# One prefetch moved, weight copies kept at other uses: eight-core macaron encoder block on Trainium2

## The chip, the cores and the metric

The kernel runs on all 8 cores of one Trainium2 chip. Each core computes one of 8 sequences by itself, with its own copy of all weights; nothing is exchanged. The metric is the device time of the slowest core, in microseconds (us). Most executions agree within 0.3%. Some fall into a second, slower state, in which the cores of one die, sometimes of both, run at a lower granted TensorE clock (0.86 in one run of the changed kernel, 0.995 to 0.998 in its others); those are left out ("fast runs" below are the others). PE is the matmul engine, DVE and ACT the vector and scalar engines, POOL and SP two further engines; here POOL issues the DMA transfers that convert f32 to bf16 on the way ("casting loads"), SP the plain ones.

## The reference, cut to what matters

```python
# x: (8, 4096, 1024) float32; D_FF = 2816, D_IN = 4608
x = x + 0.5 * swiglu(rmsnorm(x, norm_ffn1), ffn1_w_gate, ffn1_w_up, ffn1_w_down)
h = rmsnorm(x, norm_mix)
z = h @ w_in                                # q, k, v | u, v_s | gate logits
...                                         # chunked attention, spatial gating
merged = g_att * (y_att @ w_branch_att) + g_sgu * (y_sgu @ w_branch_sgu)
x = x + merged @ w_out
x = x + 0.5 * swiglu(rmsnorm(x, norm_ffn2), ffn2_w_gate, ffn2_w_up, ffn2_w_down)
return rmsnorm(x, norm_final)
```

## The kernel before

A core works through 8 tiles of 512 tokens; all matmuls are bf16. The weights do not fit into the on-chip memory. They stream through one ring buffer (RING, 46 groups of 512 columns, so about five or six chunks of up to 1 MB) in the order in which they are used. In DRAM they are f32. The first uses of a chunk load it from f32 through POOL's casting queue (1 MB written for 2 MB read). At one of these uses, which the table KEEP_AT names, the bf16 chunk is also written back from the ring to DRAM; every later use loads that copy, a plain 1 MB transfer in SP's queue. A slot of the ring is free only when its matmuls *and* its write-back are done.

```python
F2 = (3, 8, 9, 10, 2, 0, 1, 4, 5, 6, 7)     # order of the gate/up chunks
def _keep_at():                             # the use (0 = first) at which the bf16 copy is written
    at = {("ffs", 0, f2): int(n < 4) for n, f2 in enumerate(F2J)}   # gate/up of feed-forward 1
    at |= {("wds", 0, d): 1 for d in range(8)}                      # its down weights
    at |= {("wis", g): n for g, n in zip((4, 3, 2, 0, 1), (1, 0, 1, 0, 1))}     # projection
    at |= {("mgs", d): n for d, n in enumerate((0, 1, 1, 2, 0, 1, 2, 1))}       # merge
    at |= {("wos", 0): 1, ("wos", 1): 2}
    at |= {("ffs", 1, f2): n for f2, n in zip(F2, (1, 2, 0, 2, 1, 2, 1, 0, 2, 1, 2))}
    ...
def pump():                                 # issues loads while the ring has room
    ...
    if any(a < o + ng and o < b for a, b in live.values()):
        return                              # no room: the queue stops here
    ...
    if chunk not in converted:
        p.dma("pool", lambda e: e.dma_start(out=o, in_=i_), writes=res, ...)     # cast from f32
        if u >= KEEP_AT[chunk]:
            converted.add(chunk)
            pending_wb[k] = (chunk, scr, dst, i)                     # write-back follows
    else:
        p.dma("sp", lambda e: e.dma_start(out=dst, in_=scr), ...)    # the bf16 copy
```

x of a tile is 2 MB of f32, in two halves in SP's queue. The parts of the schedule that the change touches (pieces of work are yielded; a "hook" runs at a numbered piece):

```python
def dense_bank():                           # PSUM banks in turn
    b = dn[0] % n_dense[0]; dn[0] += 1
    return b
...
def down_last(t, i, fac):                   # last down product; tokens split at T_A = 320
    for d in range(2):      block(d, ALL);      nsq(t, d)
    for d in range(2, 8):   block(d, parts[0]); nsq(...)
    for d in range(2, 8):
        block(d, parts[1]); ...             # norm, apply, store of parts[0] in between
    nstat(sl=parts[1])                      # the very last norm
    ...
# main program, tile 0
run_all(main)                               # down product of tile 1 beside attention of tile 0
load_x(2)                                   # x of tile 2, ahead of the merge
...
merge(t, mh, HT, ht_m)
wh = {}                                     # hooks of the second input projection
...
win(t + 1, wh)
run_all(ffn(t, 1, False, ffn2_hooks(t)))    # second feed-forward of tile 0, all weights from f32
# next iteration: main = ffn(2, 0, ...): first feed-forward of tile 2, needs x of tile 2
```

The first feed-forward of tiles 0 and 1 is computed together, chunk by chunk, so tile 2's is only the *second* use of its weights.

Of the kernel before, what the change touches and what calls it, by code (L numbers as in the profile page):

```python
# [18 lines left out]
NT = S_LEN // T  # L19
NGR = 46  # L20
NSEM = 12
T_A = 320
N_WARM = 7
EPS = 1e-6
R_MAX = 1e18
# [7 lines left out]
def _keep_at():  # L33

    at = {("ffs", 0, f2): int(n < 4) for n, f2 in enumerate(F2J)}
    at |= {("wds", 0, d): 1 for d in range(8)}
    at |= {("wis", g): n for g, n in zip((4, 3, 2, 0, 1), (1, 0, 1, 0, 1))}
    at |= {("mgs", d): n for d, n in enumerate((0, 1, 1, 2, 0, 1, 2, 1))}
    at |= {("wos", 0): 1, ("wos", 1): 2}
    at |= {("ffs", 1, f2): n for f2, n in zip(F2, (1, 2, 0, 2, 1, 2, 1, 0, 2, 1, 2))}  # L40
    at |= {("wds", 1, d): n for d, n in enumerate((1, 2, 2, 1, 0, 2, 1, 2))}
    return at
# [173 lines left out]
def build_nc(n_tiles=NT):  # L216
# [28 lines left out]
    with ExitStack() as st:  # L245
# [63 lines left out]
        def run(p, dry):  # L309
# [222 lines left out]
            def store(t, d, sl=ALL, queue="sp"):  # L532
                b = t % 3
                h = int(sl.start > 0)
                p.dma(queue, lambda e: e.dma_start(out=out_d[t][:, d:d + 2, sl], in_=X[b][:, d:d + 2, sl]),
                      reads=[("X", b, d), ("X", b, d + 1)], writes=[("outd", d, h)], sem=f"o{d}{h}")
# [129 lines left out]
            def down_last(t, i, fac):  # L666


                b3 = t % 3
                parts = (slice(0, T_A), slice(T_A, T))  # L670
                W = [None] * 8

                def block(d, sl):
                    if not W[d]:
                        W[d] = get_slot(("wds", i, d))
                    w, wres, k = W[d]
                    by = dense_bank()
                    for fc in range(NFC):
                        p.add("pe", lambda e, fc=fc: e.matmul(  # L679
                            bank(by)[:, sl], lhsT=w[:, fc * 128:(fc + 1) * 128], rhs=HT[:, fc, sl],  # L680
                            start=(fc == 0), stop=(fc == NFC - 1)),
                            reads=wres + [("HT", fc)], writes=[rb(by)])
                    xs = X[b3][:, d, sl]
                    p.add("dve", lambda e: e.scalar_tensor_tensor(
                        out=xs, in0=bank(by)[:, sl], scalar=fac, in1=xs, op0=ALU.mult, op1=ALU.add),
                        reads=[rb(by), ("X", b3, d)], writes=[("X", b3, d)])
                    if sl.stop == T:
                        free_slot(k)

                for d in range(2):  # L690
                    block(d, ALL)
                    nsq(t, d)
                for d in range(2, 8):
                    block(d, parts[0])
                    nsq(t, d, "dve" if d > 5 else "pool", parts[0])
                for d in range(2, 8):
                    block(d, parts[1])
                    if d == 2:
                        nstat(sl=parts[0])
                    nsq(t, d, "dve" if d > 5 else "pool", parts[1])  # L700
                    if d > 2:
                        for j in range(2):
                            if 2 * (d - 3) + j < 8:
                                napply(t, 3, 2 * (d - 3) + j, parts[0])
                        if d < 7:
                            store(t, 2 * (d - 3), parts[0])
                nstat(sl=parts[1])
                for d in range(8):
                    napply(t, 3, d, parts[1])
                    if d % 2:  # L710
                        store(t, d - 1, parts[1], ("sp", "act")[d // 2 % 2])

            def ffn(t, i, use_tanh, hooks=None, narrow=False, last=False):
                hook = Hooks(hooks)
                for f2 in F2:
                    yield from gu_chunk(t, f2, get_slot(("ffs", i, f2)), "tanh" if use_tanh else "silu", hook,
                                        by_k=last and f2 == F2[0])
                if last:
                    down_last(t, i, 0.5)
                else:  # L720
                    yield from down(t, i, 0.25 if use_tanh else 0.5, hook, narrow=2 * narrow)
# [366 lines left out]
            def add_hook(hk, n, *fns):  # L1088
                hk[n] = chain(*(([hk[n]] if n in hk else []) + list(fns)))
# [14 lines left out]
            def both_hooks():  # L1104
# [5 lines left out]
                add_hook(hk, 48, const_ops)  # L1110
                return hk

            def ffn1_hooks(t):
                hk = {D1 - 2: ln_table}
                finish_hooks(hk, t - 2, 1)
                for d in range(8):
                    add_hook(hk, D1 + SQ_AT[d], P(nsq, t, d))
                return hk

            def ffn2_hooks(t):  # L1120
                hk = {}
                if t + 1 < n_tiles:
                    for s in range(4):
                        add_hook(hk, 8, P(sgu_pe, s, 4 + s))
                        add_hook(hk, 9 + 3 * s, P(sgu_out, s, 4 + s))
                if t + 2 < n_tiles:
                    for d in range(8):
                        add_hook(hk, 10 + 3 * d, P(nsq, t + 2, d, "dve" if t == 0 else "pool"))
                    add_hook(hk, 40, nstat)
                    for d in range(8):  # L1130
                        add_hook(hk, D1 + d, P(napply, t + 2, 0, d))
                if t == n_tiles - 2:
                    add_hook(hk, D1 - 2, ln_table)
                if t == n_tiles - 1:
                    for d in range(8):
                        add_hook(hk, 4 + 2 * d, P(nsq, t - 1, d))
                    finish_hooks(hk, t - 1, 22)
                    add_hook(hk, 38, flag_ops)
                if t < n_tiles - 2:
                    for d in range(8):  # L1140
                        add_hook(hk, D1 + SQ_AT[d], P(nsq, t, d))
                return hk
# [17 lines left out]
            for d in range(8):  # L1160
                add_hook(hk, SQ_AT[d], P(nsq, 0, d, "dve"))
            run_all(down(0, 0, 0.5, Hooks(hk)))
            hk = {0: nstat}
            for d in range(8):
                add_hook(hk, 1 + d // 4 * 2, P(napply, 0, 1, d))
            add_hook(hk, 3, lambda: p.add("dve", lambda e: e.tensor_copy(out=RSTD[:], in_=RS[1]),
                                          reads=[("RS", 1)], writes=["RSTD"]))
            run_all(gu_chunk(1, F2J[-1], get_slot(("ffs", 0, F2J[-1])), "raw", Hooks(hk), ht_second))
# [9 lines left out]
            for t in range(n_tiles):  # L1178
                last = t == n_tiles - 1
                mh = {}  # L1180
                if not last:
                    if t == 0:
                        main = second
                        n_dense[0] = 2
                        interleave(main, attention(t), 25, n_att(t))
                    else:
                        main = ffn(t + 1, 0, True, ffn1_hooks(t + 1), narrow=True)
                        interleave(main, attention(t), N_FFN + 16 - 3, n_att(t), 2 * NFC)
                    run_all(main)
                    if t == 0 and n_tiles > 2:  # L1190
                        load_x(2)
                    add_hook(mh, 0, nstat)
                    for d in range(8):
                        add_hook(mh, 1 + d // 2, P(napply, t + 1, 1, d))
                for d in range(8):
                    add_hook(mh, ("o", d), P(nsq, t, d))
                if last:
                    n_dense[0] = 4
                    add_hook(mh, ("o", 0), ln_table)
                    merge(t, mh, XT[(t - 1) % 2], lambda dc: ("XT", (t - 1) % 2, dc))  # L1200
                    for _ in range(3):
                        next(last_ffn)
                    nstat()
                    for d in range(8):
                        napply(t, 2, d)
                    run_all(last_ffn)
                else:
                    merge(t, mh, HT, ht_m)
                    wh = {}
                    add_hook(wh, 1, nstat)  # L1210
                    for d in range(8):
                        add_hook(wh, 3 + 2 * d, P(napply, t, 2, d))
                    win(t + 1, wh)
                if t == n_tiles - 2:
                    last_ffn = ffn(t, 1, True, ffn2_hooks(t), narrow=True)
                    interleave(last_ffn, attention(t + 1), N_FFN + 16 - 8, n_att(t + 1), 2 * NFC)
                else:
                    run_all(ffn(t, 1, False, ffn2_hooks(t), last=last))
# [122 lines left out]
```

## Time and profile before

| | before |
|---|---|
| time, median of 3 runs | 2743.96 us (2743.35 to 2861.79, the highest a slow one) |
| spans of the 8 cores in the profiled run | 2732.9 (core 3) to 2743.7 us (core 4) |
| PE busy, core 4 | 2693.3 us, 98% |
| longest wait of PE | 11.7 us, for the first weights of the second input projection |

Here is one more view, busy time by stretch, of core 3 of the kernel before. Its columns are: stretch and length; busy us (and instructions) of PE, PE's weight loads, DVE, ACT, POOL; mean granted clock of PE; mean busy share of the 16 DMA engines (in this view a full stretch shows slightly over 1); GB/s.

```profile
216.00:256.00 40.00, 38.58 (x201) 17.01 (x199) 17.79 (x36) 12.74 (x20) 7.26 (x16) 1.00 1.02 204
...
298.00:340.00 42.00, 42.00 (x196) 18.98 (x194) 22.34 (x34) 16.69 (x22) 2.18 (x4) 1.00 1.01 195
340.00:354.00 14.00, 13.28 (x61) 5.71 (x59) 6.02 (x10) 4.41 (x7) 7.82 (x8) 1.00 0.71 193
354.00:389.00 35.00, 32.19 (x150) 14.61 (x151) 12.57 (x23) 12.65 (x19) 5.23 (x11) 1.00 1.02 225
...
505.00:550.00 45.00, 44.65 (x208) 20.10 (x207) 22.56 (x34) 11.68 (x17) 1.14 (x2) 1.00 1.04 274
```

The last column but one is the one to read. From 216 to 550 us the DMA engines are full on this core but for 14 us in which they are at 0.71 (the stretches left out here show 1.01 to 1.03). In this stage, from the end of the joint first feed-forward to the first feed-forward of tile 2, weights are cast from f32 and written back at the same time.

### The profile page before, as it was taken

The page shows a single profiled execution, that of the slowest core. Times are in us where ns is not written, and L with a number is a line of the kernel's source. Part 1 is how long each engine was busy: PE and PEld are TensorE (multiplying, and loading weights), DVE is VectorE, ACT ScalarE, POOL GpSimd, SP SyncE. Part 2 cuts the span into 40 slices and gives each one's busy share as a digit, 9 for nine tenths or more (in the row PEclk, how much of TensorE's full clock was granted, in tenths as well). Part 3 has the DMA queues.
Part 4 walks back from the last instruction along what each step waited for, and adds up shares of the span by engine and source line. Part 5 has one row for each costly group of instructions (what it writes and reads, how often), then busy time and mean ns, then how long its engine had stood idle before and what let it go on. Part 6 is the DMA issues. An engine that isn't in the chain of part 4 may idle for free.

```text
span 2743.7 us, 38774 instructions; the slowest of 8 cores (2732.9 to 2743.7 us)
## 1 busy us (share of the span) xinstructions
PE 2693.3 (98%) x13174; PEld 1223.2 (45%) x13174; DVE 1180.8 (43%) x1931; ACT 911.0 (33%) x1483; POOL 336.4 (12%) x395
## 2 busy tenths in 40 slices
PE   8999989999999999999999999999999999999997
PEld 3444434444444444444444444444444444444445
DVE  5445533445334453344533445324544245454432
ACT  3313432234322343224432243322532225424321
POOL 4101120101211011110011001010010101100111
PEclk9999999999999999999999999999999999999999
DMA  9979999967797456973344634446344443443352
GB/s 190 200 128 197 193 191 180 223 226 163 181 207 234 151 153 169 241 239 134 135 154 146 215 130 139 153 146 210 132 142 152 152 171 133 146 149 127 133 185 86
DMA packets 92503, 461.95 MB, mean 168 GB/s; under 512 B 9608, under 2 KB 11656, under 8 KB 62096
## 3 DMA queue, kind: packets, MB, share of 16 engines
q1 hardware_dynamic: 68896, 361.09, 38.1%
q0 software_dynamic: 22720, 97.89, 22.5%
q8 instruction: 114, 1.87, 0.3%
q14 instruction: 85, 0.70, 0.1%
q10 hardware_dynamic: 688, 0.41, 0.0%
HBM read 488.03 MB, written 65.01 MB: 202 GB/s over the span
## 4 chain that ended last, share of the span: by engine, by line
PE 92%; DMA 3%; DVE 1%; issue 1%; ACT 1%; POOL 0%; DVEq 0%; ACTq 0%; POOLq 0%; SPq 0%
PE ps L572 43%; PE ps L645 20%; PE ps L1021 7%; PE ps L755 6%; PE ps L768 4%; PE ps L1031 4%; PE ps L1050 3%; PE ps L926 2%; PE ps L903 1%; DMA mgs<-RING 1%; PE ps L679 1%; DMA RING<-mgsrc 1%; DMA RING<-wisrc 1%; DMA X<-xT 0%; ACT E L909 0%
## 5 line engine op out<-in xcount | busy, mean ns | idle before, releaser
L572 PE MATMUL ps<-XT,RING 128*128 128x512 bf16 x5632 | 1228.2, 380 | 10.9 <-DMA RING<-fsrc 4.5
L572 PEld LDWEIGHTS ps<-XT,RING 128*128 128x128 bf16 x5632 | 548.6, 98 | 681.2 <-issue 26.9
L645 PE MATMUL ps<-HT,RING 128*128 128x512 bf16 x2480 | 567.6, 379 | 0.1
L500 POOL TENSOR_TENSOR ACC<-ACC,TG 128x512 f32<-128x512 f32 (+2 forms) x177 | 227.7, 1286 | 1698.2 <-ACT TG L497 1696.4
L594 DVE TENSOR_TENSOR HT<-ps,TG 128x512 bf16<-128x512 f32 x332 | 229.2, 691 | 424.1 <-PE ps L572 360.5
L645 PEld LDWEIGHTS ps<-HT,RING 128*128 128x128 bf16 x2480 | 235.6, 98 | 286.2 <-issue 24.5
L497 ACT ACTIVATE TG<-X 128x512 f32<-128x512 f32 (+2 forms) x230 | 140.6, 615 | 328.9 <-DVE X L657 232.1
L1021 PE MATMUL ps<-XT,RING 128*128 128x512 bf16 x1024 | 242.0, 379 | 0.0
L579 ACT ACTIVATE TG<-ps 128x512 f32<-128x512 f32 x154 | 92.0, 597 | 394.4 <-PE ps L572 374.1
L585 ACT ACTIVATE TG<-ps 128x512 f32<-128x512 f32 x154 | 91.8, 597 | 365.7 <-PE ps L572 354.8
L581 DVE SCALAR_TENSOR_TENSOR TG<-TG,ps 128x512 f32<-128x512 f32 x154 | 105.8, 687 | 238.0 <-ACT TG L579 196.9
L909 ACT ACTIVATE E<-ps 128x1024 bf16<-128x1024 f32 (+3 forms) x156 | 152.8, 985 | 105.8 <-PE ps L903 102.3
L914 DVE TENSOR_TENSOR E<-E,EB 128x1024 bf16<-128x1024 bf16 (+1 forms) x240 | 119.1, 500 | 139.2 <-ACT E L909 127.9
L755 PE MATMUL ps<-XT,RING 128*128 128x512 bf16 x768 | 168.9, 379 | 0.0
L1021 PEld LDWEIGHTS ps<-XT,RING 128*128 128x128 bf16 x1024 | 99.6, 98 | 120.8 <-issue 3.2
L1035 DVE SCALAR_TENSOR_TENSOR TG<-TG,ps 128x512 f32<-128x512 f32 x128 | 87.3, 686 | 153.2 <-PE ps L1031 116.7
L657 DVE SCALAR_TENSOR_TENSOR X<-ps,X 128x512 f32<-128x512 f32 x104 | 71.7, 691 | 184.7 <-PE ps L645 183.4
L1026 ACT ACTIVATE TG<-ps,BG 128x512 f32<-128x512 f32 x128 | 87.2, 687 | 189.2 <-PE ps L1021 176.9
L523 DVE SCALAR_TENSOR_TENSOR XT<-X,G,RSTD 128x512 bf16<-128x512 f32 x176 | 124.5, 746 | 46.3 <-ACT RSTD L516 46.3
L768 PE MATMUL ps<-RING,XT 128*128 128x512 bf16 x512 | 116.1, 383 | 12.3 <-DMA RING<-wisrc 11.7
L755 PEld LDWEIGHTS ps<-XT,RING 128*128 128x128 bf16 x768 | 74.9, 98 | 90.2
L1050 PE MATMUL ps<-HT,RING 128*128 128x512 bf16 x448 | 99.0, 379 | 2.4 <-DVE HT L1040 2.4
(111 smaller groups left out, 1626.5 us busy)
## 6 DMA issues: line engine op xcount, KB each, us to landing
RING<-ffs SPq DMA_DIRECT2D x126, 1024.0 KB, 4.9
RING<-wds SPq DMA_DIRECT2D x93, 704.0 KB, 4.3
RING<-mgs SPq DMA_DIRECT2D x48, 768.0 KB, 4.2
RING<-wis SPq DMA_DIRECT2D x32, 1024.0 KB, 4.9
RING<-fsrc POOLq DMA_DIRECT2D x29, 1024.0 KB, 16.2
RING<-wd POOLq DMA_DIRECT2D x35, 704.0 KB, 15.3
ffs<-RING SPq DMA_DIRECT2D x22, 1024.0 KB, 13.0
out<-X SPq DMA_DIRECT2D x28, 512.0 KB, 5.3
```

The costliest lines, as they stand in the source:

```text
L497: p.add("act", lambda e: e.activation(out=buf[:, sl], in_=src, func=AF.Square, scale=1.0 / 32.0), reads=[xres], writes=[bres])
L500: p.add(eng, lambda e: e.tensor_tensor(out=acc, in0=acc, in1=buf[:, sl], op=ALU.add), reads=["ACC", bres], writes=["ACC"])
L523: p.add("dve", lambda e: e.scalar_tensor_tensor(out=dst, in0=src, scalar=G4[:, which * 8 + d:which * 8 + d + 1], in1=RSTD[:, sl], op0=ALU. ...
L572: p.add("pe", lambda e: e.matmul(bank(b), lhsT=Wc[:, kc * 512 + j * 128:kc * 512 + (j + 1) * 128], rhs=xt[:, kc, :], start=(kc == 0), stop ...
L594: p.add("dve", lambda e: e.tensor_tensor(out=dst, in0=bank(bu), in1=buf[:], op=ALU.mult), reads=[rb(bu), bres], writes=[dres])
L645: p.add("pe", lambda e, n=n, fc=fc, W=W, by=by, hap=hap: e.matmul(bank(by), lhsT=W[:, fc * 128:(fc + 1) * 128], rhs=hap, start=(n == 0), s ...
L755: p.add("pe", lambda e, kc=kc, W=W, b=b, cc=cc: e.matmul(bank(b), lhsT=W[:, kc * 512 + cc * 128:kc * 512 + (cc + 1) * 128], rhs=XT[t % 2][ ...
L768: p.add("pe", lambda e, kc=kc, W=W, b=b, s=s: e.matmul(bank(b), lhsT=XT[t % 2][:, kc, s * 128:(s + 1) * 128], rhs=W[:, kc * 512:(kc + 1) * ...
L909: p.add("act", lambda e, j=j, sl=sl, qa=qa, col=ok_col(): e.activation(out=E[:, sl, :, qa:T], in_=PS[1 + j][:].rearrange("p (h c) -> p h c ...
L914: p.add("dve", lambda e, sl=sl, q0=q0, q1=q1, u0=u0: e.tensor_tensor(out=E[:, sl, :, q0:q1], in0=E[:, sl, :, q0:q1], in1=EB[:, 2 * hp:2 * ...
L1021: p.add("pe", lambda e, kc=kc, W=W, bgt=bgt, j=j: e.matmul(bank(bgt), lhsT=W[:, j * 1024 + kc * 128:j * 1024 + (kc + 1) * 128], rhs=XT[t % ...
L1050: p.add("pe", lambda e, dc=dc, W=W, by=by, d4=d4: e.matmul(bank(by), lhsT=W[:, (d4 * 8 + dc) * 128:(d4 * 8 + dc + 1) * 128], rhs=m[:, dc, ...
```

## The change

Its intent: take the 11.7 us before the second projection away by moving the 2 MB of x out of the merge and by writing fewer copies there; shorten the first norm, the start of the last feed-forward and the end of the program; and give gate, up and down fixed PSUM bank parity.

```diff
-T_A = 320
+T_A = 256
+D_SPLIT = 3
...
-    at |= {("wds", 0, d): 1 for d in range(8)}
-    at |= {("wis", g): n for g, n in zip((4, 3, 2, 0, 1), (1, 0, 1, 0, 1))}
-    at |= {("mgs", d): n for d, n in enumerate((0, 1, 1, 2, 0, 1, 2, 1))}
+    at |= {("wds", 0, d): int(d > 3) for d in range(8)}
+    at |= {("wis", g): n for g, n in zip((4, 3, 2, 0, 1), (0, 1, 1, 0, 1))}
+    at |= {("mgs", d): n for d, n in enumerate((1, 2, 1, 2, 3, 1, 2, 3))}
...                                     # down_last: 3 columns whole, then 5 twice in halves
             def ffn(t, i, use_tanh, hooks=None, narrow=False, last=False):
                 hook = Hooks(hooks)
+                if narrow:
+                    dn[0] += (2 - dn[0]) % 4
...
-                        add_hook(hk, 10 + 3 * d, P(nsq, t + 2, d, "dve" if t == 0 else "pool"))
+                        add_hook(hk, 10 + 3 * d if t else 20 + 2 * d, P(nsq, t + 2, d, ...))
...
-            hk = {0: nstat}             # first half kernel: norm one group later
+            hk = {1: nstat}
...
-                    if t == 0 and n_tiles > 2:
-                        load_x(2)
...
+                    silu_table()        # last feed-forward: table early, six PSUM banks
+                    next(last_ffn)
...
+                    n_dense[0] = 6
...
                     for d in range(8):
                         add_hook(wh, 3 + 2 * d, P(napply, t, 2, d))
+                    if t == 0 and n_tiles > 2:
+                        add_hook(wh, 8, P(load_x, 2))
                     win(t + 1, wh)
```

More of the change, by code (lines that the diff above doesn't have):

```diff
@@ L688, in block @@
                         free_slot(k)
-                for d in range(2):
+                for d in range(D_SPLIT):
                     block(d, ALL)
                     nsq(t, d)
-                for d in range(2, 8):
+                for d in range(D_SPLIT, 8):
                     block(d, parts[0])
                     nsq(t, d, "dve" if d > 5 else "pool", parts[0])
-                for d in range(2, 8):
+                for d in range(D_SPLIT, 8):
                     block(d, parts[1])
-                    if d == 2:
+                    if d == D_SPLIT:
                         nstat(sl=parts[0])
                     nsq(t, d, "dve" if d > 5 else "pool", parts[1])
-                    if d > 2:
-                        for j in range(2):
-                            if 2 * (d - 3) + j < 8:
-                                napply(t, 3, 2 * (d - 3) + j, parts[0])
-                        if d < 7:
-                            store(t, 2 * (d - 3), parts[0])
+                    if d > D_SPLIT:
+                        for j in (0, 1):
+                            napply(t, 3, 2 * (d - D_SPLIT - 1) + j, parts[0])
+                        store(t, 2 * (d - D_SPLIT - 1), parts[0])
                 nstat(sl=parts[1])
@@ L1111, in both_hooks, with silu_table @@
                 return hk
+            def silu_table():
+                p.add("act", lambda e: e.activation(out=ASTAT[:, 3:4], in_=EPSB[:], func=AF.Silu),
+                      reads=["EPSB"], writes=[("as", 3)])
             def ffn1_hooks(t):
@@ L1127, in ffn2_hooks @@
                     for d in range(8):
-                        add_hook(hk, 10 + 3 * d, P(nsq, t + 2, d, "dve" if t == 0 else "pool"))
+                        add_hook(hk, 10 + 3 * d if t else 20 + 2 * d, P(nsq, t + 2, d, "dve" if t == 0 else "pool"))
                     add_hook(hk, 40, nstat)
@@ L1131, in ffn2_hooks @@
                         add_hook(hk, D1 + d, P(napply, t + 2, 0, d))
-                if t == n_tiles - 2:
+                if t >= n_tiles - 2:
                     add_hook(hk, D1 - 2, ln_table)
@@ L1162, in run @@
             run_all(down(0, 0, 0.5, Hooks(hk)))
-            hk = {0: nstat}
+            hk = {1: nstat}
             for d in range(8):
-                add_hook(hk, 1 + d // 4 * 2, P(napply, 0, 1, d))
+                add_hook(hk, 3, P(napply, 0, 1, d))
             add_hook(hk, 3, lambda: p.add("dve", lambda e: e.tensor_copy(out=RSTD[:], in_=RS[1]),
@@ L1203, in run @@
                     nstat()
-                    for d in range(8):
+                    silu_table()
+                    next(last_ffn)
+                    for d in range(7):
                         napply(t, 2, d)
                     run_all(last_ffn)
+                    napply(t, 2, 7)
+                    n_dense[0] = 6
                 else:
```

## The prediction

> **What bounds the kernel now.** I read the busy shares first. PE is busy 98% of a span of 2743.7 us on the slowest core, so all that any reordering can win is the other 2%: 2743.7 - 2693.3 = 50.4 us, part of it a start and an end that no kernel avoids.
>
> ```profile
> PE 2693.3 (98%) x13174; PEld 1223.2 (45%) x13174; DVE 1180.8 (43%) x1931; ACT 911.0 (33%) x1483; POOL 336.4 (12%) x395
> ```
>
> The second line of the chain that ended last says that this is not an accident of one window: 43% of the span is the gate and up product (L572), 20% the down product (L645), and DMA only 3%.
>
> Next the waits of PE (who released it, us in total, times, longest). The reader is to see that a single wait is 11.7 us, that one of three is 4.8 us, and that the rest is crumbs.
>
> ```profile
> PE ps L768 <- DMA RING<-wisrc: 11.7, 1, 11.7
> PE ps L512 <- DVE ACCR L503: 6.6, 3, 4.8
> PE ps L903 <- ACT E L909: 4.6, 8, 0.6
> ...
> PE ps L572 <- ACT TG L585: 1.5, 1, 1.5
> PE ps L572 <- DVE X L657: 1.5, 2, 1.3
> ```
>
> Then PE's timeline (start, us, what, idle before it) to place them. The 11.7 us stand at the head of the second input projection; 1.60 us in the first half kernel; 1.26, 0.22 and 1.52 us at the start of the last feed-forward; 4.82 us before the very last norm.
>
> ```profile
> 207.37 0.47 PE L512 MATMUL ps<-ACCR,ONESR 128*128 128x512 f32 x1 [1.60 <-DVE ACCR L503]
> ...
> 366.20 5.07 PE L768 MATMUL ps<-RING,XT 128*128 128x512 bf16 x16 [11.73 <-DMA RING<-wisrc]
> ...
> 2612.37 0.38 PE L572 MATMUL ps<-XT,RING 128*128 128x512 bf16 x1 [1.26 <-DVE X L657]
> 2612.96 6.42 PE L572 MATMUL ps<-XT,RING 128*128 128x512 bf16 x29 [0.22 <-DVE X L657]
> 2620.91 32.97 PE L572 MATMUL ps<-XT,RING 128*128 128x512 bf16 x152 [1.52 <-ACT TG L585]
> ...
> 2734.68 0.50 PE L512 MATMUL ps<-ACCR,ONESR 128*128 128x192 f32 x1 [4.82 <-DVE ACCR L503]
> ```
>
> Where the 11.7 us come from is in the chain of waits, in order of time. A merge load ends at 313; the write-back of that same merge weight (its bf16 copy, to DRAM) takes 35 us; only then is its ring slot free and the weights of the projection can be loaded, another 17 us.
>
> ```profile
> 287.77 25.51 DMA RING<-mgsrc
> 313.34 35.11 DMA mgs<-RING
> 349.04 16.93 DMA RING<-wisrc
> ```
>
> The write-back is 768 KB; elsewhere such a chunk lands in 4.2 us. Ahead of it in SP's queue stand the two 1 MB loads of x of tile 2, issued at 298.6, which took 37.6 us. The DMA table for 240 to 480 us shows why: the engines are full, 80.3% of their time in POOL's casting loads and 18.3% in SP's queue.
>
> **What the Trainium skill says.** "TensorE: Matmul & The Clock Gate", section "Single matmul latency", gives about 216 ns between matmuls of 512 columns. The trace agrees: 72.54 us for 336 of them, 215.9 ns. So PE's work is at its floor. "DMA: Bandwidth & Descriptors", section "Queues, rings and completion order", says that each engine goes round its queues packet by packet and takes one ring's descriptors in order. The trace agrees: at 300 to 312 us POOL's queue has 86.1% and SP's 15.0%, and the write-back ends after the x loads ahead of it. "ScalarE: Activation LUTs", section "What ACT_TABLE_LOAD costs", has 1283 ns for a load plus a drain of 1380; the trace has 1.28 us and the ACTIVATE directly after it, so I count 1.28.
>
> **The change part by part.**
>
> *Loads.* x of tile 2 moves from before the first merge to the ninth piece of the second projection (about 16 us into it), and no merge weight is written back in tile 0 (two were). The first weights of the second projection now come from their bf16 copy through SP's queue instead of a casting load. Both links of the chain above go. Per core, the span less its wait there (0 to 7): 2735.0 - 3.2, 2742.2 - 9.6, 2739.1 - 6.1, 2732.9 - 3.2, 2743.7 - 11.7, 2739.7 - 7.5, 2741.5 - 10.6, 2733.7 - 2.6 (core 7 waits for a norm sum there, POOL being stuck behind the same load). The slowest becomes core 2 with 2733.0. Gain: 2743.7 - 2733.0 = 10.7 us, not 11.7.
>
> What it costs elsewhere, in DMA time: POOL's queue moved 29.54 MB in 80.3% of 240 us, 153 MB per ms; SP's 16.06 MB in 18.3%, 365 MB per ms. A 704 KB down weight is thus 4.7 us from f32 and 2.0 from the copy. Four of them are now kept at their first use, in a stage with slack (share 0.55 at 137 to 165 us): in the full stage four loads fall by 2.7 us each and four write-backs of 2.0 us leave. Seven more merge loads from f32 in tiles 1 to 3 cost 5.1 - 2.1 = 3 us of DMA each, in windows with shares of 0.40 to 0.80. I count them as hidden.
>
> *First half kernel.* The norm sum stands one group of 8 matmuls later (1.73 us), so the 1.60 us before it go. But the eight applies now follow both gate evictions: the second silu waits for a table load until about 213.2, its product until 214.0, then 8 x 0.685 = 5.5 us: the last XT at 219.5 against 220.2 before. Gain 0.7.
>
> *Last feed-forward.* The silu table is loaded early (1.28 us off) and six PSUM banks instead of four let the second chunk start without the first one's eviction: the 1.52 us go. The 1.26 + 0.22 us stay nearly whole: the first chunk takes banks 0 to 3, down column 7 is in bank 1, its product ends at 2610.5, and its eviction still stands behind seven applies of 0.67 us begun at about 2606.7: done at 2612.0. Gain 1.6.
>
> *End.* Now 3 columns whole, then 5 blocks of 256 tokens twice (before: 2, then 6 of 320 and 192). PE's work is the same. Before, the eviction of column 7 waited 2.67 us for a store of the other tokens of that same column (tracked as one tile). In the new order that store comes after the eviction. From PE's last product (2729.8) to the norm sum was 4.9 us; now 0.1 + 0.43 + 0.1 + 0.42 + 0.1 + 0.42 + 0.1 = 1.7. Against this, ln and exp take 0.13 more and eight applies 8 x (0.43 - 0.34) = 0.7 more, a larger store 0.2. 3.2 - 1.0 = 2.2, and 0.2 of waiting before the first half's sum goes. Gain 2.4.
>
> *Bank parity.* Before, the down product began in the bank of the first gate, free for long; now in that of the second, whose last reader ends at 594.48 where PE wants it at 594.43. With about 0.1 us for the semaphore: 0.15 us in each of 7 such places. Loss 1.0. The 0.6 us of the attention waits are four exps of 1.02 us in a row on ACT; parity does not touch them.
>
> Sum: 10.7 + 0.7 + 1.6 + 2.4 - 1.0 = 14.4 us. I take back 1.5 us for what the first rival leaves: 2744.0 - 14.4 + 1.5 = 2731.
>
> **The rivals.** (1) *The wait moves on.* SP's queue in the second projection now holds 2 MB of x and then the write-back of its last weight; the fifth gate chunk of the next feed-forward needs that slot. x and the write-back are about 8.5 us of DMA time, and at 15% of the engines that is over 50 us, too late by 10 to 20. Against it: once POOL is blocked its queue empties and SP's gets everything, so by my count they end near 399, and the chunk lands at about 407 to 415 for a need at 417. Also, the stall itself gave DMA 11.7 us to catch up, which it now lacks. In full this rival gives 2738 to 2745. (2) *Nothing at the projection, small gains only:* had the wait come from saturated engines and not from order, the 10.7 us would reappear later and only some 4 us remain: 2740. Against it: DMA work falls by about 20 us in that stage, and cores 0, 3 and 7 wait only 3 us with the same bytes. (3) *POOL becomes the bound of the later merges* through more casting loads of 5.1 us per 5.2 us of PE: then 3 to 10 us in tiles 1 to 3, 2735 to 2741. Shares there speak against it. (4) *The tail pays more than counted:* at most 2 us.
>
> **Range and chances.** All gains whole, with nothing lost to parity: 2744 - 15.4 = 2728.6; a few us below that if other cores' small waits go too: low end 2725. A good part of rival 1 or 3: high end 2741. Two per cent is 55 us, more than all idle time of PE, so faster by that is all but impossible; slower would need 55 us of new stalls. Faster 0.01, same 0.97, slower 0.02.
>
> **What would show it.** Right: no wait on projection weights on any core; no 35 us write-back; 1.3 to 1.5 us still before the third or second matmul of the last feed-forward, none at its second chunk; the last norm's wait at 1.5 to 2.0; spans of the cores within 5 us of each other. Wrong: a PE wait for f32 gate weights at some 30 to 60 us after the second projection starts, or for merge weights in tiles 1 to 3; idle time before the last applies.

## The result, and the profile after

| | before | after |
|---|---|---|
| median of 4 runs each | 2744.5 us | 2746.59 us (2742.38 to 3137.87) |
| median of the fast runs alone | 2743.96 us | 2745.97 us |
| ratio of fast runs, 95% interval | | 1.0004 (0.9981 to 1.0027) |
| spans of the cores, profiled run | 2732.9 to 2743.7 | 2727.7 (core 7) to 2745.7 (core 3) |

All ratios here are the mean time of one kernel's fast runs over that of the other's of the same rounds, so not quite the ratio of the quoted medians; the times given below after "Measured" are medians of the fast runs. The change moved nothing that these runs can see: its time is some 15 us above the predicted 2731, and above the high end of 2741. Was nothing gained, or was something gained and lost again? The busy line and the waits of PE on the slowest core (core 3; in the changed kernel most lines have numbers one higher) answer it.

```profile
PE 2697.4 (98%) x13152; PEld 1223.5 (45%) x13152; DVE 1179.5 (43%) x1930; ACT 911.0 (33%) x1484; POOL 338.6 (12%) x397
```

```profile
PE ps L573 <- DMA RING<-fsrc: 18.9, 6, 6.5
PE ps L904 <- ACT E L910: 4.8, 9, 0.6
PE ps L1051 <- DVE HT L1041: 2.1, 7, 0.3
PE ps L513 <- DVE ACCR L504: 1.8, 1, 1.8
PE ps L573 <- DVE X L658: 1.2, 1, 1.2
```

The wait for wisrc, the projection weights, is gone, on every core. The last norm's wait fell from 4.8 to 1.8. In the place of the first stands a wait for fsrc, f32 gate weights. Some of its 18.9 us lie at the start of the program and are old; PE's timeline of core 3 shows the new ones, and the two small places predicted at the end.

```profile
532.79 8.44 PE L573 MATMUL ps<-XT,RING 128*128 128x512 bf16 x32 [6.52 <-DMA RING<-fsrc]
547.32 51.14 PE L573 MATMUL ps<-XT,RING 128*128 128x512 bf16 x224 [6.09 <-DMA RING<-fsrc]
...
2617.93 39.66 PE L573 MATMUL ps<-XT,RING 128*128 128x512 bf16 x183 [1.22 <-DVE X L658]
...
2735.01 0.36 PE L513 MATMUL ps<-ACCR,ONESR 128*128 128x256 f32 x1 [1.83 <-DVE ACCR L504]
```

6.5 and 6.1 us of waiting, at 526 and 541 us: that is tile 2's first feed-forward, four of whose chunks are cast from f32 a second time. And the waits cost more than their length. Undisturbed, 32 of these matmuls take 7.07 us and 224 take 48.51 (both durations stand in other cores' and runs' lines); here they took 8.44 and 51.14, so 1.37 + 2.63 = 4.0 us went in slow restarts. With 0.2 us of waiting at 453, core 3 lost 16.8 us between 450 and 600.

The stretches of core 3 after, same columns as before:

```profile
216.00:256.00 40.00, 38.52 (x198) 16.86 (x198) 18.28 (x37) 11.91 (x19) 4.74 (x11) 1.00 0.85 183
...
298.00:340.00 42.00, 42.00 (x197) 19.00 (x195) 22.09 (x33) 16.19 (x22) 3.87 (x7) 1.00 0.90 159
340.00:354.00 14.00, 13.71 (x64) 6.08 (x63) 6.22 (x9) 4.27 (x7) 5.91 (x5) 1.00 0.66 118
354.00:389.00 35.00, 35.00 (x163) 15.89 (x162) 14.19 (x26) 13.88 (x21) 7.56 (x15) 1.00 1.02 204
389.00:430.00 41.00, 41.00 (x218) 18.94 (x217) 16.28 (x32) 8.96 (x14) 3.17 (x6) 1.00 0.97 198
...
505.00:550.00 45.00, 32.40 (x138) 13.79 (x137) 17.16 (x26) 9.29 (x13) 0.78 (x1) 0.88 1.05 238
```

Before 354 us the engines now have time to spare: 40 x 0.15 + 42 x 0.10 + 14 x 0.34 = 15.0 us idle, against 14 x 0.29 = 4.1 before. After 354 us they are nearly as full as before (0.97 from 389 to 430 us here, 0.95 to 0.98 on the eight cores, elsewhere 1.02 and more on this core), and x of tile 2 now lies there. The 15.0 us are not the table's alone: with x put back (first experiment) the same stretches of core 3 leave 9.7 us idle (0.82 in the first and the last), so some 5.3 us of them are x itself, and 5.6 us the new table's gain over the 4.1. POOL's timeline says why the spare time is not used, and SP's line where x is:

```profile
240.94 0.53 POOL L371 DMA_DIRECT2D RING<-wd  x1 [22.23 <-PE ps L769]
...
330.75 0.54 POOL L371 DMA_DIRECT2D RING<-wisrc  x1 [14.47 <-PE ps L1032]
...
376.35 0.54 POOL L371 DMA_DIRECT2D RING<-fsrc  x1 [6.37 <-PE ps L769]
387.69 0.77 POOL L371 DMA_DIRECT2D RING<-fsrc  x1
407.13 1.62 POOL L371 DMA_DIRECT2D RING<-fsrc  x3 [18.67 <-DMA wis<-RING]
...
453.63 1.60 POOL L371 DMA_DIRECT2D RING<-wd  x3 [13.90 <-DMA ffs<-RING]
```

```profile
370.71 1.24 SPq L410 DMA_DIRECT2D X<-xT  x2
372.04 0.89 SPq L386 DMA_DIRECT2D wis<-RING  x1
```

Up to 376 us POOL waits for *PE*, 22.2 and 14.5 us at a time: every slot of the ring holds weights that PE has not yet used, so no load can start, however idle the engines. From 387 us POOL waits 18.7 us for a *write-back*: that of the projection weight, issued just behind x in SP's queue. This looks exactly like the first rival of the prediction. A second stand, of 13.9 us here and 8.8 to 13.9 us on the eight cores, ends at 447 to 454 us, behind the write-back of a gate chunk of the second feed-forward (ffs). Whether a stand is the cause was the question for the experiments.

### The profile page after: what moved, and what is told of

Same layout as the page of the kernel before. It is cut to its first block, busy times and chain, and to the rows that moved or that the text cites. A ratio compares the mean times of both kernels' runs of the same rounds, so it can differ in the third digit from the quotient of the medians.

```text
span 2745.7 us, 38680 instructions; the slowest of 8 cores (2727.7 to 2745.7 us)
## 1 busy us (share of the span) xinstructions
PE 2697.4 (98%) x13152; PEld 1223.5 (45%) x13152; DVE 1179.5 (43%) x1930; ACT 911.0 (33%) x1484; POOL 338.6 (12%) x397
## 4 chain that ended last, share of the span: by engine, by line
PE 94%; DMA 2%; DVE 1%; issue 1%; ACT 1%; POOL 0%; DVEq 0%; ACTq 0%; POOLq 0%; SPq 0%
PE ps L573 42%; PE ps L646 20%; PE ps L1022 8%; PE ps L756 6%; PE ps L1032 4%; PE ps L769 4%; PE ps L1051 4%; PE ps L927 2%; DMA RING<-fsrc 1%; PE ps L904 1%; PE ps L680 1%; DMA X<-xT 1%; ACT E L910 0%; DVE XT L524 0%; PE ps L844 0%
## 5 line engine op out<-in xcount | busy, mean ns | idle before, releaser
L573 PE MATMUL ps<-XT,RING 128*128 128x512 bf16 x5632 | 1232.9, 381 | 22.4 <-DMA RING<-fsrc 18.9
L501 POOL TENSOR_TENSOR ACC<-ACC,TG 128x512 f32<-128x512 f32 (+1 forms) x176 | 228.2, 1297 | 1607.4 <-ACT TG L498 1606.7
L498 ACT ACTIVATE TG<-X 128x512 f32<-128x512 f32 (+1 forms) x229 | 140.5, 616 | 326.7 <-DVE X L658 232.5
```

Source lines behind the costliest of these rows:

```text
L498: p.add("act", lambda e: e.activation(out=buf[:, sl], in_=src, func=AF.Square, scale=1.0 / 32.0), reads=[xres], writes=[bres])
L501: p.add(eng, lambda e: e.tensor_tensor(out=acc, in0=acc, in1=buf[:, sl], op=ALU.add), reads=["ACC", bres], writes=["ACC"])
L573: p.add("pe", lambda e: e.matmul(bank(b), lhsT=Wc[:, kc * 512 + j * 128:kc * 512 + (j + 1) * 128], rhs=xt[:, kc, :], start=(kc == 0), stop ...
```

## The experiments

Two theories. **Queue:** x stands ahead of a write-back in SP's queue; the slot comes free late, POOL stands still, and the loads behind it never catch up. Then another order or another queue mends it. **Budget:** the DMA engines are all but full from 354 to 550 us; x's 2 MB (at the 365 GB/s of the plain queue that the prediction works out, an estimate of 5.7 us of all engines) were moved into that stretch from one where the engines had idle time; anything full-size there costs, in whatever queue or order. Then only moving work out of the stretch helps. Eleven kernels ran, on three chips; all gave correct results.

### x back ahead of the merge

```diff
 # on the changed kernel
                     run_all(main)
+                    if t == 0 and n_tiles > 2:
+                        load_x(2)
...
-                        add_hook(wh, 8, P(load_x, 2))
```

> The changed kernel with the load of x of tile 2 put back before the first merge; all else as changed. Place theory (x in the second projection costs what the copies won): POOL's 18.7 us stand behind the projection write-back shrinks to under 8 us, PE's wait for f32 gate weights at 520 to 550 us falls from 12.8 us on the slowest core to under 4 us, no wait for projection weights returns, time 2730 to 2735 us. Table theory (the new table of copies itself overloads the engines, x is innocent): that wait stays at 10 us or more, time 2742 to 2748 us. A middle case, x delaying the copy of the first projection weight that now stands behind it in SP's queue: a wait of 2 to 8 us at the head of the second projection.

Measured: 2730.62 us (fast runs 2730.34 to 2730.71), ratio to before 0.9946 (0.9922 to 0.997). Spans of the cores 2726.1 to 2729.1. No core waits for any weight between 300 and 700 us. The windows and PE's timeline of core 3:

```profile
298.00:340.00 42.00, 41.70 (x194) 18.80 (x193) 22.10 (x34) 16.43 (x22) 2.68 (x5) 1.00 1.02 207
340.00:354.00 14.00, 14.00 (x67) 6.34 (x66) 5.82 (x9) 5.26 (x9) 8.13 (x7) 1.00 0.82 224
...
505.00:550.00 45.00, 45.00 (x210) 20.38 (x209) 22.58 (x35) 11.65 (x17) 0.00 (x0) 1.00 1.00 264
```

```profile
505.59 72.69 PE L573 MATMUL ps<-XT,RING 128*128 128x512 bf16 x336
```

x fills idle time of the merge (shares 1.02 and 0.82 in place of 0.90 and 0.66), neither of POOL's two stands is there (no core pauses over 7.5 us from 385 to 500 us), and all 336 matmuls of tile 2's gate and up product run without a break. So the move of x, alone of all parts, took the gain away. It does not yet tell queue from budget.

### x behind the write-back

```diff
-                        add_hook(wh, 8, P(load_x, 2))
+                        add_hook(wh, 12, P(load_x, 2))
```

> The changed kernel with the load of x of tile 2 four pieces (about 7 us) later, so that in SP's queue it stands behind the write-back of the last projection weight and no longer ahead of it; the same bytes in the same stage. Queue theory (x ahead of the write-back holds the ring slot): POOL no longer stands 18.7 us, PE's wait for f32 gate weights at 520 to 550 us falls below 5 us, time 2731 to 2736 us. Budget theory (the engines are full from 366 us on, and x is some 6 us of work more there whatever the order): POOL's stand goes but PE's wait stays within 3 us of the changed kernel's, time 2741 to 2747 us.

Two fast runs, 2743.46 and 2748.82 us, and two slow ones. By the trace, every core still waits 5.1 to 9.6 us for fsrc at 523 to 545 us, five of them 2.1 to 3.2 us more in sum before that, at 439 to 463 us, and POOL still stands still, now 23 to 24 us, which the view puts down on four cores to the *next* write-back, that of a gate chunk (ffs). The order in the queue was changed and the loss stayed: a miss for the queue theory in its narrow form. But neither theory had expected POOL to stand, and the longer stand cost engine time (shares of 0.90 to 0.94 from 389 to 430 us), so this run doesn't decide between them.

### x in another queue

```diff
-            def load_x(t, paced=True):
+            def load_x(t, paced=True, queue="sp"):
...
-                        add_hook(wh, 8, P(load_x, 2))
+                        add_hook(wh, 8, P(load_x, 2, False, "act"))     # ACT issues it
```

> The changed kernel with x of tile 2 loaded at the same place but issued by ACT, so in a ring of its own: no write-back stands behind it in SP's queue, the bytes and the stage are the same. Queue theory (x ahead of write-backs holds ring slots, POOL stands 19 to 24 us behind one): the stands fall under 10 us and PE's waits for f32 gate weights at 420 to 550 us fall below 5 us in sum, time 2731 to 2736 us. Budget theory (the engines are full from 354 us to 550 us and x adds its 6 us there whoever issues it): PE's waits stay at 7 us or more on the slowest cores, time 2738 to 2747 us.

Measured: 2745.47 us, ratio 0.9994 (0.9975 to 1.0013). Issued at 367 to 370 us by ACT (368 to 372 by SP before), x no longer stands ahead of the projection's write-back, the 17 to 19 us stand is gone on all cores, and the engines are full from 389 to 430 us (1.00 or more). The waits came all the same, as large as before (core 7):

```profile
451.83 1.61 POOL L371 DMA_DIRECT2D RING<-wd  x3 [12.86 <-DMA ffs<-RING]
```

```profile
530.30 9.77 PE L573 MATMUL ps<-XT,RING 128*128 128x512 bf16 x32 [4.80 <-DMA RING<-fsrc]
546.91 51.44 PE L573 MATMUL ps<-XT,RING 128*128 128x512 bf16 x224 [6.84 <-DMA RING<-fsrc]
```

The queue theory falls as it was put: without the stand that it blames, the loss is the same. The second stand, behind ffs, is still there (12.9 us on core 7, 9.5 to 13.3 on the eight cores).

### Half of x early

```diff
+                    if t == 0 and n_tiles > 2:
+                        load_x(2, True, (0,))                           # first half before the merge
...
-                        add_hook(wh, 8, P(load_x, 2))
+                        add_hook(wh, 8, P(load_x, 2, True, (4,)))       # second half in the projection
```

> The changed kernel with one half of x of tile 2 loaded before the first merge and the other half in the second projection. Budget theory: the late work falls from some 5.7 us of engine time to half, so PE's waits for f32 gate weights at 420 to 550 us, some 12 us on the slowest core with all of x late and none with x early, come to about half or less, 2 to 7 us; time 2732 to 2739 us. If it were a threshold of order alone (anything of x ahead of the copies holds the slot), they stay above 8 us: 2741 us or more.

Measured: 2741.35 us, ratio 0.9978 (0.9959 to 0.9998). The mean of the cores' waits is 4.2 us in place of 7.2, in line with half the bytes; but the slowest core still waits 9.9 us, which I had not expected. The time follows the slowest core, so half the bytes bought less than half the loss. By the figures of the expectation (over 8 us, 2741 us or more) this run fell on the side of its rival, that anything of x ahead of the copies holds the slot; the cores that wait nothing (0, 3, 4, 6) had POOL standing 12 to 14 us at that place all the same.

### Two other copies taken out of the stretch

x stays late, as changed. Two gate chunks of the *second* feed-forward are kept at their second use (tile 1) instead of their first: two write-backs of 1 MB leave the full stretch, just as many bytes as x brought in.

```diff
-    at |= {("ffs", 1, f2): n for f2, n in zip(F2, (1, 2, 0, 2, 1, 2, 1, 0, 2, 1, 2))}
+    at |= {("ffs", 1, f2): n for f2, n in zip(F2, (1, 2, 1, 2, 1, 2, 1, 1, 2, 1, 2))}
```

> The changed kernel, x late as there, but two of the second feed-forward's weights are kept one tile later, so two write-backs of 1 MB (some 2.9 us of engine time each by the rate of SP's queue) leave the full stage of tile 0. Budget theory: about as much leaves as x brought, PE's waits at 420 to 550 us fall from 12 us to 5 us or less on the slowest core; time 2731 to 2738 us, unless the two extra casting loads make a new wait in tile 1's second feed-forward at 740 to 860 us. If x itself is what hurts (its 2 KB packets, its place ahead of the projection's copy), the waits stay at 9 us or more.

Measured: 2731.81 us, ratio 0.9946 (0.9922 to 0.997). x is still late and still ahead of the projection's write-back. Core 5, POOL and then PE:

```profile
405.70 1.62 POOL L371 DMA_DIRECT2D RING<-fsrc  x3 [18.61 <-DMA wis<-RING]
```

```profile
532.72 48.51 PE L573 MATMUL ps<-XT,RING 128*128 128x512 bf16 x224 [0.79 <-DMA RING<-fsrc]
```

POOL stands 18.6 us behind the same write-back, as long as in the changed kernel, and PE waits 0.8 us where core 5 of the changed kernel waited 5.5 and 3.6. This stand is harmless once the two write-backs are gone. New waits, 0.6 to 1.6 us in sum on five cores, appear at 817 to 838 us, in tile 1, where the two copies are now made.

One thing weakens this evidence. Of the two write-backs taken out (issued at 392 and some 438 us on core 3 of the changed kernel) the later is the one behind which POOL makes its *second* stand, and with it this stand is gone on every core (no pause over 6.9 us at 430 to 460 us). In the runs of the table below the two go together: each core on which POOL stands 10 us or more at 438 to 454 us waits 2.9 us or more at 520 to 550 us, and no other core waits over 1.2 us there. So this run can't tell the bytes of the two write-backs from the ring slots that they held. What speaks for the bytes is that the engines lose no time in the second stand (shares of 1.01 to 1.06 on the eight cores of the changed kernel from 439 to 447 us), and that x early ends the stand without touching these write-backs: it looks like a sign of the backlog. A run that takes 2 MB out of the stretch elsewhere would have settled it.

The PE waits for weights from 300 to 700 us, added up per core in us, one profiled execution each:

| kernel | core 0 | 1 | 2 | 3 | 4 | 5 | 6 | 7 |
|---|---|---|---|---|---|---|---|---|
| before | 3.2 | 10.1 | 6.1 | 3.6 | 11.7 | 7.5 | 10.6 | 0.4 |
| after | 2.9 | 9.3 | 6.1 | 12.8 | 7.7 | 9.1 | 9.9 | 0 |
| x in ACT's queue | 9.6 | 0.7 | 9.9 | 3.2 | 6.1 | 11.1 | 3.0 | 11.8 |
| half of x early | 0 | 6.4 | 9.3 | 0 | 0 | 9.9 | 0 | 7.7 |
| two copies later | 0 | 0 | 0 | 0.4 | 0 | 1.1 | 0 | 0 |
| x early | 0 | 0 | 0 | 0 | 0 | 0 | 0 | 0 |

With half of x exactly one core of each pair of neighbours (0 and 1, 2 and 3, ...) waits in this execution. Which of the two it is changes from run to run, and the pattern isn't strict: in another run of that kernel the spans of cores 0 to 3 all lie between 2731.9 and 2736.5 us, where cores that don't wait have 2726 to 2728.

### The parts alone, on the kernel before

Only the new table of copies (x and everything else as before):

> The kernel before with the new table of copies alone. Place theory: the wait of 11.7 us at the head of the second projection goes (2 us or less, up to 8 if the copy's load waits behind x), nothing of more than 4 us comes at 520 to 550 us, time 2734 to 2738 us. Table theory: PE waits 10 us or more for f32 gate weights at 520 to 550 us, time 2742 to 2748 us.

Measured: 2734.77 us, ratio 0.9962 (0.9942 to 0.9981), no waits for weights from 300 to 700 us on any core. The table by itself brings the whole gain at the projection.

Only x moved to the projection (and the sums of squares that read it), old table:

> The kernel before with x of tile 2 loaded in the second projection (and its squares moved as in the change), the old table of copies. Place theory: the write-back of the merge weight no longer has x ahead of it and takes under 20 us, the wait at the head of the projection falls below 4 us, but PE waits 8 to 20 us at 520 to 550 us: time 2741 to 2750 us. Table theory: the first wait falls and nothing comes in its place, time 2733 to 2738 us.

Its two quickest runs (2776.16 and 2776.74 us) have cores 4 and 5, in the second also 0 and 1, at a granted clock of 0.984 to 0.986. On the undisturbed cores of the profiled one (2739.7 to 2748.6 us) the projection's wait is gone, and waits of 6.4 to 10.6 us in sum stand at 528 to 549 us. So moving x alone cures the projection too, and pays for it 170 us later.

Only the merge row of the table, and only the row of the first feed-forward's down weights:

> The kernel before with the new copies of the merge weights alone (no merge weight written back in tile 0). Slot theory (the wait of 11.7 us comes from the write-back that holds a ring slot behind x): the wait at the head of the second projection falls to 3 us or less, time 2734 to 2737 us. Load theory (it comes from too much casting before the projection, which the early copies of four down weights take away): it stays at 6 us or more, time 2740 to 2745 us.

> The kernel before with the four early copies of down weights alone (some 19 us of engine time less in the full stage), merge weights still written back in tile 0 behind x. Slot theory: the write-back is still held up by x, the wait at the projection stays at 4 us or more on the slowest cores, time 2737 to 2744 us. Load theory: with the engines less full x and the write-back both end sooner, the wait is under 2 us, time 2733 to 2736 us.

Too few fast runs (2742.19 and 2741.13; 2748.04 and 2747.8 us). The traces still tell something: *either* row by itself takes the projection's wait away on all cores, so that wait hung on little; and neither suffices at 530 us: two cores still wait there with the merge row (8.2 and 2.8 us), four with the other (6.3 to 10.7). Each run gave the waits at the projection of one theory (slot with the first, load with the second) and neither the times. That it is the sum that counts fits this, but isn't shown by it.

Only the three small parts (first norm, last feed-forward, end), without table, x and parity:

> The kernel before with the parts that touch no weight: the later norm sum in the first half kernel, the early silu table and six banks in the last feed-forward, the tail in halves; no bank rotation. The wait at the head of the second projection stays (up to 12 us on the slowest core). By the traces of the changed kernel these are worth 0.85, 2.0 and 1.8 us, so 2739 to 2741 us where the kernel before has 2744 to 2747; if the parts are worth nothing when alone, 2744 us or more.

Measured: 2740.72 us, ratio 0.9978 (0.9954 to 1.0002); the interval holds the 4.7 us predicted for the three together, and also no gain at all; the terms are read from the traces in the next section. The projection's wait is all there, core 7 of this kernel:

```profile
347.36 1.15 POOL L371 DMA_DIRECT2D RING<-wisrc  x2 [32.26 <-DMA mgs<-RING]
```

```profile
364.64 5.18 PE L767 MATMUL ps<-RING,XT 128*128 128x512 bf16 x16 [10.99 <-DMA RING<-wisrc]
```

### x early, and no bank parity

```diff
 # on the version with x ahead of the merge
                 hook = Hooks(hooks)
-                if narrow:
-                    dn[0] += (2 - dn[0]) % 4
```

> The changed kernel with x of tile 2 back before the first merge and without the bank rotation ahead of the feed-forwards that share with attention; a candidate for the best version. If the rotation costs what the prediction said (0.15 us at 7 places), PE's waits on banks there go and the time is 1 to 2 us under the run with x early alone: 2728.5 to 2730 us. If the rotation gains, it is 2731 us or more.

Measured: 2728.24 us (fast runs 2727.91 to 2729.25), ratio 0.9937 (0.9921 to 0.9953); spans 2723.6 to 2726.4. This is the lowest time, below both kernels. From one merge to the next (tiles 1 to 2) it takes 336.67 us on all 8 cores, as the kernel before does; with parity, on all 8 cores, 336.97. The 0.30 us are found where a down product starts behind the gate and up product. PE on core 3, before, and then after:

```profile
1231.73 25.41 PE L572 MATMUL ps<-XT,RING 128*128 128x512 bf16 x117
1256.99 2.54 PE L645 MATMUL ps<-HT,RING 128*128 128x512 bf16 x11
```

```profile
1249.79 22.61 PE L573 MATMUL ps<-XT,RING 128*128 128x512 bf16 x104
1272.53 2.53 PE L646 MATMUL ps<-HT,RING 128*128 128x512 bf16 x11
```

Matmuls are pipelined, so without a wait the next group starts before the modelled end of the last: 1231.73 + 25.41 = 1257.14, and the down product starts 0.15 us earlier. After, the end is at 1272.40 and the down product starts 0.13 us *later*: 0.28 us together. What it waits for is the reader of the bank that parity gives it, on DVE:

```profile
1271.59 0.69 DVE L582 SCALAR_TENSOR_TENSOR TG<-TG,ps 128x512 f32<-128x512 f32 x1 [1.78 <-PE ps L573]
```

It ends at 1272.28, just when PE would have started (1272.25), and PE starts 0.25 us after it.

## Why the prediction was wrong

**The wait at the projection: right.** It is gone on all cores, as is the chain of write-back and reload before it, and the table alone gained about 10 us (ratio 0.9962 of 2746), close to the 10.7 predicted for table and x together. One cost was left out: the restart. Before, the 16 matmuls after the wait took 5.07 us on core 4 against 3.62 undisturbed, so that core lost 13.2 us there, not 11.7. The Trainium skill, "TensorE: Matmul & The Clock Gate", section "What's actually happening", says that the clock halves after about 3.4 us of idling, in a free-running window, and comes back after as long a busy one. The traces agree in the main: in the runs of the table every wait of over 3.4 us was followed by slow matmuls, none of under 2 us was, and in between it went either way (3.19 us on core 0 before: 15 in 5.16 us; 3.24 on core 3: 16 in 3.61). The edge isn't sharp: outside the table, waits of 3.77 us (core 3, x behind the write-back) and 3.94 us (core 7, x moved alone) were followed by 224 matmuls at full speed, in 48.51 us, and one of 1.97 us (core 4, x behind the write-back) by slow ones, 224 in 50.19. The prediction also took 4.2 us as what a chunk of 768 KB takes elsewhere; that is the median of the loads of these chunks, while their write-backs have a median of 8.6 us.

**The step that failed** is the cost of the move of x, for which the sum had only the 1.5 us taken back for rival 1, and with it the answer to the second rival: "*DMA work falls by about 20 us in that stage*". It may well have fallen so; but the stage was treated as one pot. Before 354 us the engines of core 3 had 10.9 us more idle time than before (15.0 - 4.1; some half of it is x's own departure), and the full ring kept POOL from using it; x fell after 354 us, where the engines were at 0.97 and more. PE then waited 12.6 us on the slowest core for f32 gate weights at 526 to 547 us, and lost 4.0 us more in slow restarts. The prediction said of the stall itself that it "gave DMA 11.7 us to catch up, which it now lacks" and did not follow this to the end of the stage, where the last chunks cast from f32 are needed. That x's new place is the cause is shown by x early, which differs from the changed kernel in nothing else. That x's place ahead of the write-back in SP's queue is not what hurts is shown by two kernels (other queue, two copies later). That it is the engines' time is what the shares and three kernels point to (x early, half of x early, two copies later); the ring slots held by the two ffs write-backs remain a rival that no run separates from it.

**Rival 1, "The wait moves on"**, was right that it would, and wrong about where and why. The write-back behind x ended at 407 (core 3), against the 399 counted; yet the chunk that needed its slot was in time, with no wait of PE near 417. The wait came 110 us later. **Rival 2** ("the 10.7 us would reappear later") is what happened: it had 2740, the fast runs 2746. It was dismissed because cores 0, 3 and 7 waited only 3 us with the same bytes; the table above has unequal waits in every kernel that waits at 530 us, so they were no sign against it. **Rival 3**, POOL as the bound of later merges, did not occur.

**The small terms, sized against the traces of core 4 before and core 3 after:**

| term | predicted | measured |
|---|---|---|
| first half kernel, gate chunk to last matmul that waits for XT | 0.7 | 16.42 - 15.57 = 0.85 |
| last feed-forward, start of the down product before it to start of the last | 1.6 | 90.02 - 88.02 = 2.0 |
| end, start of the last down product to the end | 2.4 | 52.9 - 51.1 = 1.8 |
| bank parity, loss | 1.0 (7 x 0.15) | 2.0 (7 x 0.28, measured at one place) |

The wait of 1.2 us after the first matmuls of the last feed-forward stays and the one at its second chunk goes, both as said. The end fell short by 0.6, because a store came in the way once more: an apply waits 0.60 us for it. Parity cost twice what was predicted per place: the reader ends where the prediction put it, some 0.03 us too late, but from its end to PE's start it took 0.25 us, not "about 0.1 us for the semaphore". The versions with and without parity differ by 2730.62 - 2728.24 = 2.4 us, on two chips.

So with x left where it was, the prediction's 2731 would have been close to the measured 2730.6, though partly by luck, since errors offset: parity cost 1 us more than counted, and the 1.5 us taken back for rival 1 were not needed. The move of x cost some 15 us (2745.97 - 2730.62, not measured side by side).

**What stays open.** Whether the late write-backs hurt by their bytes or by the slots that they hold, as said above. And why one core of a pair waits and the other doesn't. The Trainium skill, "HBM Reference", section "Specifications (TRN2)", says that two cores share one memory domain's bandwidth; a core that falls behind could so leave its neighbour more. The table's pattern agrees with it in the main, but no run tested it: this is argued, not shown.

## What to carry to other kernels

Before moving a transfer, make a table of DMA share by stage, and ask in which stage the bytes leave and in which they arrive: here two megabytes moved out of a stage with idle engines into a full one undid ten microseconds of gain, some 150 us later. Transfer time that was saved where the ring of buffers was full did not help here until it was filled with something that needs no slot, the prefetch of x. When a blocked queue looks like the cause, run a kernel that leaves it blocked and lightens the load, and check that the lightening frees no other blocked place: here that kernel was as fast as the cure, but it had removed a second stand too.

## What the Trainium skill lacked or had wrong

- "TensorE: Matmul & The Clock Gate", section "Back-to-back issue gap", gives some 131 ns for each 512-column matmul of a sustained stream and calls 216 ns the isolated figure. In all these traces the sustained figure is 216: 336 matmuls, each with its weight load, in 72.69 us, 216.3 ns.
- "ScalarE: Activation LUTs", section "What ACT_TABLE_LOAD costs", adds a drain of 1380 ns to the load. The traces have the load alone, 1.28 us, with the next ACTIVATE 0.02 us behind it.
- "DMA: Bandwidth & Descriptors" has no rate for loads that cast. Here POOL's casting queue wrote 153 GB/s of bf16 over the time that its packets took, against 365 GB/s in the plain queue, so a copy that is read instead of a cast saves more than half of the engines' time.
- No page says that transfer time saved while a prefetch ring is full can be lost (10.9 us more idle engine time here, about half of it from moving x), or that of two neighbouring cores one may wait 6 to 10 us in a full stage while the other waits none.
